# Gates of a hybrid encoder layer in three pieces, their tiles in the mixers' pool, and the decay rows stored through GpSimd's queue

## The chip, the cores and the metric

The kernel runs on one core of a Trainium2 chip. The metric is the device time of one execution in microseconds (us), the median of several. The engines are TensorE (PE, matmuls; PEld, its weight loads), VectorE (DVE), ScalarE (ACT), GpSimd (POOL) and SyncE (SP). Each engine works through its own instructions strictly in order; SP does nothing but issue DMA transfers, and GpSimd can issue them too.

## The reference

One layer of an encoder is computed for 1024 frames of a new stream (the prompt) and 32 frames of a running one (the sample), model width 1024, all in float32. What matters here is the input projection and what its gate columns feed:

```python
mod = jax.nn.silu(c) @ w_ada + b_ada                  # conditioning, 6 x 1024 columns
h = x * (1 + sc1) + sh1
mq, mk, mv, mo, mi, mf, fq, fk, fv, ff, gu, gv = split(h @ w_in)
li = mi + b_mlstm_i                                   # 4 heads
lf = log_sigmoid(mf + b_mlstm_f)                      # 4 heads
logf = log_sigmoid(ff + b_fox_f)                      # 8 heads, an output too
# forgetting attention (FoX), 8 heads of width 64
Ft = cumsum(logf, axis=1)
logits = q @ k.T * scale + Ft[query] - Ft[key]        # causal
hf = softmax(logits) @ v
# mLSTM, 4 heads, chunks of 64: running maxima m of b - b' + li, b = cumsum(lf)
w_intra = exp(dmat - m); w_inter = exp(m0 + b - m)
```

The mLSTM and the attention outputs join a gated MLP's, go through an output projection and a layer norm, then a SwiGLU feed-forward and another layer norm. Outputs besides the result are the attention's keys, values and log forgets, and the mLSTM's states C, n and m.

## The kernel before

Float32 products are made of two float32r parts: a weight tile `raw` (512 KB) is cast to `whi` on ACT (L105) and the rest `wlo` is formed on DVE (L106); each product then takes three matmuls (L117 to L119, and L282 to L284 with the operands' roles exchanged). Activations `h1h` and `h1l` are split likewise.

The program is written in one order, and a scheduler gives each engine its own, by when it expects an instruction's inputs and buffers to be there. First comes the conditioning (`ada`, L179: small matmuls, each unit with two loads of 512 KB into the two buffers `late`), the first projection, and two units of value columns (`tm_unit`) whose last 8 columns are the gate inputs, gathered in `G`. Then `gates()` runs, then a table `ORDER` names the rest of this stage: `q` is the projection of one attention head's queries and keys (`head_unit`, for heads 0 and 1 with further columns by `fm_unit`'s body), `f` is that head's attention on the first 512 rows, `k` the mLSTM's key projection, `v`, `o`, `a` further projections and conditioning units, `s` the mLSTM's states, `m` one mLSTM chunk. `f` and `m` have raised priority.

`gates()` does, in this order: a log-sigmoid on a tile of 128 partitions x 9 x 12 (DVE, a polynomial, with one ACT exp); four matmuls that make cumulative sums (L484 to L487); a matmul for the totals of earlier tiles (L497); the decay rows `fr`, 6 per head and tile, high and low parts and ones, stored to DRAM as `dfs` by two stores on SP; a running maximum in 7 steps (L512); a serial recurrence over 8 tiles (L525) between two tiny matmuls (L521 and L529); the columns `col` through four transposes (L547); and stores of `o_lf`, `dM`, `dd0` and the end states. Its tiles lie in a pool of their own, on the right of the memory, closed at its end. The pool `mx0`, of which the attention's and the mLSTM's tiles come, is opened after that.

A head's projection goes to one of three PSUM banks `g`. It is emptied by ACT and DVE into the tiles `qp`, `k1`, `k2`, `q2` (L399 to L404) and, for the output `o_kT`, through two small buffers `qkr` (L407; L368 and L424 use them too, and each waits until the store of an earlier user has landed). The tiles `q2` and `k2` get 4 rows each from `dfs` by loads on SP (`decay`). A score takes two matmuls: L768 needs the head's own tiles, L769 also the decay rows. L777 is the softmax's exp, L804 the transposes, L812 to L821 the products with the values.

Of the kernel before, what the change touches and what calls it, by code (L numbers as in the profile page):

```python
# [7 lines left out]
F32 = mybir.dt.float32  # L8
F32R = mybir.dt.float32r
AF = mybir.ActivationFunctionType  # L10
ALU = mybir.AluOpType
# [4 lines left out]
P = 128  # L16
# [4 lines left out]
NS = 32  # L21
# [14 lines left out]
T1 = (1, 1, 0, 2)  # L36
# [2 lines left out]
MLB = (1, 2, 3, 4, 5)  # L39
RESE = "pp"  # L40
TAFF = ("aaaaaaaa", "aaaaaaav")
ORDER = "q0 f0 q1 a f1 a q2 f2 k0 k1p s a q3 f3 a v q4 f4 a q5 f5 o a m0 q6 f6 a m1 q7 m2 f7 a m3"
ADAPOS = 4
GENG = (0, 1, 1, 0)
FP = (0, 0)
# [8 lines left out]
NEG = -1e30  # L54
# [11 lines left out]
def f(ap):  # L66
    return ap.bitcast(F32)


class Kernel:  # L70
# [10 lines left out]
    def t(self, pool, shape, dt=F32, tag=None, bufs=None):  # L81
        self.n += 1
        kw = {} if bufs is None else {"bufs": bufs}
        return pool.tile(shape, dt, tag=tag, name=f"{self.phase}_{tag}_{self.n}", **kw)
# [2 lines left out]
        self.lastload = self.nc.sync.dma_start(out, in_)  # L87
        return self.lastload

    def store(self, out, in_):  # L90
        self.nc.sync.dma_start(out, in_)


    def weights(self, src, nk, ncol, eng=None):
# [334 lines left out]
    def gates(self):  # L429
        self.phase = "gates"  # L430
        nc, d = self.nc, self.d
        ctx = ExitStack()
        gp = self.pool("gates", ctx=ctx, side="right")
        t = lambda shape, tag, dt=F32: self.t(gp, shape, dt, tag)
        R = 36
        ut = t([64, 64], "ut")
# [5 lines left out]
        ind, sel, back = t([R, 9], "ind"), t([R, 4], "sel"), t([4, R], "back")  # L442
# [10 lines left out]
        m0 = t([4, 9], "m0")  # L453
        nc.vector.memset(m0[:, 0:1], NEG)
        mm = t([4, 2, 9], "mm")
# [5 lines left out]
        a, e, s, s2, p = (t([P, 9, 12], f"g{i}") for i in range(5))  # L461
# [11 lines left out]
        ls = t([P, 9, 12], "ls")  # L473
# [3 lines left out]
        gi, gm, gn, gf = (t([P, 9, n], f"gw{i}") for i, n in enumerate((4, 4, 4, 8)))  # L477
# [11 lines left out]
        rf = t([72, P], "rf")  # L489
        nc.scalar.copy(rf, ps[:72, 256:384])  # L490
        nc.vector.tensor_copy(scan[0][:, 64:192], ps[:R, 0:128])
        rs = t([R, 4, P], "rs")
        nc.scalar.copy(rs[:, 0, :], ps[:R, 0:128])
        b = t([R, P], "gb")
# [3 lines left out]
        fc = t([64, 1], "fc")  # L498
        nc.vector.tensor_copy(fc, pc[:64, 0:1])
        ft = t([64, P], "ft")  # L500
# [3 lines left out]
        nc.vector.tensor_scalar(fr[:, 0:2, :], f(fr[:, 4:6, :]), -1.0, None, ALU.mult)  # L504
# [9 lines left out]
        E = t([R, 2], "E")  # L514
# [4 lines left out]
        EI = t([R, 2, 9], "EI")  # L519
        nc.vector.tensor_tensor(EI, E.unsqueeze(2).to_broadcast([R, 2, 9]), pair(ind), ALU.mult)  # L520
        nc.tensor.matmul(pc[:4, 32:50], sel, EI.rearrange("p a j -> p (a j)"), start=True, stop=True)  # L521
        ab = t([4, 2, 9], "ab")
        nc.vector.tensor_copy(ab, pc[:4, 32:50].rearrange("p (a j) -> p a j", a=2))
        for j in range(8):
            nc.vector.scalar_tensor_tensor(m0[:, j + 1:j + 2], ab[:, 0, j:j + 1], m0[:, j:j + 1], ab[:, 1, j:j + 1],  # L525
# [1 line left out]
        nc.vector.tensor_copy(mm[:, 0, 0:8], m0[:, 0:8])  # L527
        nc.vector.tensor_tensor(mm[:, 1, :], mm[:, 0, :], ab[:, 0, :], ALU.max)
        nc.tensor.matmul(pc[:R, 64:82], back, mm.rearrange("p a j -> p (a j)"), start=True, stop=True)  # L529
        mt, mc = t([R, 2, 9], "mt"), t([R, 2], "mc")  # L530
        nc.vector.tensor_tensor(mt, pc[:R, 64:82].rearrange("p (a j) -> p a j", a=2), pair(ind), ALU.mult)
        nc.vector.tensor_reduce(mc, mt, AX.X, ALU.add)
        M = t([R, P], "M")
# [4 lines left out]
        self.store(self.dM, M)  # L538
        self.store(d["o_m"], m0[:, 8:9])
        mes, d0 = t([4, 1], "mes"), t([4, 9], "d0")  # L540
        nc.vector.tensor_tensor(mes, mm[:, 1, 8:9], ab[:, 1, 8:9], ALU.add)
        self.store(d["o_ms"], mes)
        nc.vector.tensor_tensor(d0, mm[:, 0, :], mm[:, 1, :], ALU.subtract)
        self.store(self.dd0, d0)
# [757 lines left out]
    def run(self):  # L1302
        nc, tc, d = self.nc, self.tc, self.d
        dr = self.pool("dr", space=DRAM)
        t = lambda shape, tag: self.t(dr, shape, F32, tag)
# [60 lines left out]
        self.tm_unit(w1[0], 264, self.evac_v(0))  # L1366
        more(T1[1])
        self.tm_unit(w1[1], 264, self.evac_v(1))
        more(T1[2])
        self.gates()  # L1370
        more(T1[3])
        s2 = ExitStack()
        self.mx = self.pool("mx0", ctx=s2)
        self.foxbufs = (2, 2, 2, 2, 3)
        self.heads = {}

        def emit(x):
            eng = nc.gpsimd if x[-1] == "p" else nc.vector
            x = x.rstrip("p")
            i = int(x[1:] or 0)  # L1380
            if x[0] == "f":
                return self.fox(i, ((0, 1, 2, 3),))
            if x[0] == "m":
                return self.mlstm(i)
            if x[0] == "q":
                self.head_unit(i)
            elif x[0] == "k":
                self.fm_unit(w3[i], self.evac_mqk(2 + i, 0.125), eng=eng)
            elif x[0] == "s":
                self.mlstm_states()  # L1390
            elif x[0] == "a":
                more(1)
            else:
                self.tm_unit(w2["-vo".index(x)], 256, self.evac_raw((None, self.dmv, self.dmo)["-vo".index(x)]), eng=eng)
            return ()

        for x in ORDER.split():
            if x[0] in "fm" and HPA:
                with tc.high_priority(HPA):
                    weave(*[iter(emit(y)) for y in x.split("+")])  # L1400
            else:
                weave(*[iter(emit(y)) for y in x.split("+")])
# [119 lines left out]
        n = nj * 256  # L1522
        t = self.t(self.pz, [P, 4, n], F32R, "z0", 1)
        w = self.last_weights(((t[:, 0], t[:, 1]), (t[:, 2], t[:, 3])), (2, 3))
        act2 = dict(act)
        for half, (a, b) in enumerate(LN[1][::-1]):
# [6 lines left out]
            else:  # L1533
                h, l = (self.t(pb, [P, KT * 272], F32R, f"{x}{a}", 1) for x in ("ah", "al"))
# [111 lines left out]
```

## Time and profile before

| | |
|---|---|
| time, median of 3 runs (lowest, highest) | 1389.02 us (1388.13, 1390.63) |
| profiled execution: time, span | 1390.74 us, 1389.0 us |
| mean granted clock of TensorE | 0.988 |
| busy in the span: PE, DVE, ACT, POOL | 97%, 73%, 47%, 17% |
| where the stage stands in the span | first gate instruction on DVE (L459) at 108.66 us, projection of head 4 from 228.6 us on |

A row of the profile names line, engine, operation, output and input tiles without buffer numbers. "Granted clock" is the share of full speed that TensorE's throttle allowed. A busy PE sets the pace; idle time of another engine costs nothing unless PE waits for it.

### The profile page before, as it was taken

What the parts mean: (1) busy time and instruction counts of PE and PEld (TensorE: products, weight loads), DVE (VectorE), ACT (ScalarE), POOL (GpSimd) and SP (SyncE); (2) the same over time, 40 slices, a digit from 0 to 9 for tenths busy, and PEclk for the clock granted to TensorE, in tenths of its full rate; (3) what the DMA queues carried; (4) which work ended last, traced back from release to release, by engine and by line L of the source; (5) the groups of instructions that cost most, each with busy time, mean ns of one, the idle gap of its engine ahead of it and who ended that gap; (6) DMA issues with size and microseconds to landing.
All of it is one profiled execution on the core that took longest, in us unless ns stands there. A gap on an engine that the chain in (4) does not pass through costs nothing.

```text
span 1389.0 us, 25227 instructions
## 1 busy us (share of the span) xinstructions
PE 1341.3 (97%) x9432; PEld 1224.2 (88%) x9432; DVE 1013.7 (73%) x2144; ACT 653.7 (47%) x1274; POOL 236.2 (17%) x269
## 2 busy tenths in 40 slices
PE   7997999999999899999999999999999999999996
PEld 4896899988899778888887889899999999999996
DVE  5546643678779757777776766677998988888777
ACT  3313444553545544545544445345574554545355
POOL 1000100032156600000000000264610000000341
PEclk9999899999999999999999999999999999999998
DMA  9764664455765665444443442564597768463321
GB/s 360 252 225 122 187 186 129 128 170 157 224 202 159 171 199 182 125 131 137 135 134 86 107 127 80 187 171 133 160 239 188 214 165 212 139 175 112 102 91 65
DMA packets 123513, 224.65 MB, mean 162 GB/s; under 512 B 21260, under 2 KB 66232, under 8 KB 123392
## 3 DMA queue, kind: packets, MB, share of 16 engines
q1 hardware_dynamic: 118080, 212.95, 49.4%
q0 software_dynamic: 5168, 9.96, 4.6%
q8 instruction: 74, 1.21, 0.4%
q14 instruction: 47, 0.39, 0.1%
q10 hardware_dynamic: 144, 0.14, 0.0%
HBM read 191.21 MB, written 51.72 MB: 175 GB/s over the span
## 4 chain that ended last, share of the span: by engine, by line
PE 83%; DVE 7%; DMA 4%; ACT 2%; issue 2%; SPq 1%; POOL 1%; DVEq 0%; ACTq 0%; POOLq 0%
PE up_g L117 5%; PE up_g L118 5%; PE up_g L119 5%; PE dn_g L119 4%; PE dn_g L117 4%; PE dn_g L118 4%; PE sup_u L119 3%; PE sup_u L117 3%; PE sup_u L118 3%; PE tm_g L283 3%; PE tm_g L282 2%; PE tm_g L284 2%; PE wo_g L119 2%; PE wo_g L117 2%; PE wo_g L118 2%; PE fox_t L804 2%
## 5 line engine op out<-in xcount | busy, mean ns | idle before, releaser
L117 PE MATMUL up_g<-mlstm_ah,up_whi 128*128 128x512 f32 (+1 forms) x384 | 142.2, 371 | 5.1 <-ACT lna_tmp L1053 3.3
L118 PE MATMUL up_g<-mlstm_al,up_whi 128*128 128x512 f32 (+1 forms) x384 | 142.2, 370 | 0.4 <-DVE mlstm_al L1058 0.4
L119 PE MATMUL up_g<-mlstm_ah,up_wlo 128*128 128x512 f32 (+1 forms) x384 | 141.3, 368 | 0.0
L283 PE MATMUL tm_g<-tm_wlo,start_h1h 128*128 128x256 f32 (+1 forms) x384 | 109.4, 286 | 0.9 <-DVE tm_wlo L106 0.9
L282 PE MATMUL tm_g<-tm_whi,start_h1h 128*128 128x256 f32 (+1 forms) x384 | 109.1, 286 | 0.3 <-DVE tm_traw L352 0.2
L284 PE MATMUL tm_g<-tm_whi,start_h1l 128*128 128x256 f32 (+1 forms) x384 | 109.1, 285 | 0.0
L1177 ACT CAST sup_whi<-sup_raw 128x1024 fp32r<-128x1024 f32 x54 | 56.0, 1048 | 91.0 <-PE dn_u L118 47.6
L117 PEld LDWEIGHTS up_g<-mlstm_ah,up_whi 128*128 128x128 f32 x384 | 73.6, 192 | 17.5 <-ACT mlstm_ah L1057 3.5
L118 PEld LDWEIGHTS up_g<-mlstm_al,up_whi 128*128 128x128 f32 x384 | 73.7, 192 | 11.9 <-DVE mlstm_al L1058 1.1
L119 PEld LDWEIGHTS up_g<-mlstm_ah,up_wlo 128*128 128x128 f32 x384 | 73.8, 192 | 10.8
L777 ACT ACTIVATE fox_p<-fox_s,fox_fmx 128x384 f32<-128x384 f32 (+2 forms) x96 | 55.2, 579 | 57.2 <-DVE fox_fmx L775 43.6
L105 ACT CAST up_whi<-up_raw 128x1024 fp32r<-128x1024 f32 x50 | 52.4, 1048 | 61.6 <-PE dn_g L118 20.9
L1032 DVE SCALAR_TENSOR_TENSOR wo_z<-dn_g,start_mod,wo_z 128x512 f32<-128x512 f32 (+4 forms) x120 | 60.2, 519 | 22.5 <-PE dn_g L119 22.0
L1178 DVE TENSOR_TENSOR sup_wlo<-sup_raw,sup_whi 128x1024 fp32r<-128x1024 f32 x54 | 68.1, 1264 | 10.8 <-ACT sup_whi L1177 10.8
L106 DVE TENSOR_TENSOR up_wlo<-up_raw,up_whi 128x1024 fp32r<-128x1024 f32 x50 | 66.8, 1336 | 12.3 <-ACT up_whi L105 11.6
L283 PEld LDWEIGHTS tm_g<-tm_wlo,start_h1h 128*128 128x128 f32 x384 | 72.2, 188 | 2.6 <-issue 1.2
L282 PEld LDWEIGHTS tm_g<-tm_whi,start_h1h 128*128 128x128 f32 x384 | 72.1, 189 | 1.8 <-DVE tm_traw L352 0.7
L117 PE MATMUL dn_g<-up_acth,dn_whi 128*128 128x512 f32 (+2 forms) x200 | 73.5, 368 | 0.0
L118 PE MATMUL dn_g<-up_actl,dn_whi 128*128 128x512 f32 (+2 forms) x200 | 73.3, 368 | 0.0
L119 PE MATMUL dn_g<-up_acth,dn_wlo 128*128 128x512 f32 (+2 forms) x200 | 73.3, 366 | 0.0
L284 PEld LDWEIGHTS tm_g<-tm_whi,start_h1l 128*128 128x128 f32 x384 | 72.2, 188 | 0.5 <-issue 0.4
L105 ACT CAST dn_whi<-dn_raw 128x1024 fp32r<-128x1024 f32 (+1 forms) x44 | 42.7, 971 | 51.0 <-PE up_g L118 11.4
(641 smaller groups left out, 4605.5 us busy)
## 6 DMA issues: line engine op xcount, KB each, us to landing
up_raw<-w_gu SPq DMA_DIRECT2D x50, 512.0 KB
dn_raw<-w_dn SPq DMA_DIRECT2D x28, 512.0 KB
ada_late<-w_ada SPq DMA_DIRECT2D x24, 512.0 KB
wo_raw<-w_o SPq DMA_DIRECT2D x24, 512.0 KB
sup_raw<-w_gu SPq DMA_DIRECT2D x20, 512.0 KB
start_dp<-w_gu SPq DMA_DIRECT2D x19, 512.0 KB
start_dp<-w_gu POOLq DMA_DIRECT2D x19, 512.0 KB, 7.2
sup_raw<-start_dp SPq DMA_DIRECT2D x18, 512.0 KB
```

The lines of the kernel that those rows point to most:

```text
L105: nc.scalar.copy(hi[:, :w], raw[:, :w])
L106: (eng or nc.vector).tensor_tensor(lo[:, :w], raw[:, :w], f(hi[:, :w]), ALU.subtract)
L117: nc.tensor.matmul(ps, hi, xh(k), start=start and k == 0, stop=False)
L118: nc.tensor.matmul(ps, hi, xl(k), start=False, stop=False)
L119: nc.tensor.matmul(ps, lo, xh(k), start=False, stop=stop and k == n - 1)
L282: nc.tensor.matmul(ps[:, :ncol], xh, hi, start=k == 0, stop=False)
L283: nc.tensor.matmul(ps[:, :ncol], xh, lo, start=False, stop=False)
L284: nc.tensor.matmul(ps[:, :ncol], xl, hi, start=False, stop=k == 7)
L777: nc.scalar.activation(pr[:, lo:hi], banks[x][:, :hi - lo], AF.Exp, bias=mxs[:, 0:1], accum_out=sums[:, x:x + 1])
L1032: self.lastz = self.nc.vector.scalar_tensor_tensor(z[:, m, x:y], ps[:, x - a:y - a], g[i], z[:, m, x:y], ALU.mult, ALU.add)
L1177: nc.scalar.copy(h, x)
L1178: tt(l, x, f(h), ALU.subtract)
```

## The change

`gates()` becomes a generator in three parts. The first runs where `gates()` ran and ends with the decay rows; the second, the mLSTM's part, is named in `ORDER` as `g` behind head 0's attention; the third, with the stores of `o_lf`, `dM`, `dd0` and the end states, is a second `g` further back. The decay rows are two tiles now, queries and keys, stored by four DMAs on GpSimd's queue in place of two on SP's. The gates' tiles are taken from the mixers' pool `mx0`, under the names of mLSTM tiles (many small ones as slices of one tile `mo`), so that pool is opened before the gates.

```diff
-ORDER = "q0 f0 q1 a f1 a q2 f2 k0 k1p s a q3 f3 a v q4 f4 a q5 f5 o a m0 q6 f6 a m1 q7 m2 f7 a m3"
+ORDER = "q0 f0 g q1 a f1 a g q2 f2 k0 k1p s a q3 f3 a v q4 f4 a q5 f5 o a m0 q6 f6 a m1 q7 m2 f7 a m3"
...
-    def store(self, out, in_):
-        self.nc.sync.dma_start(out, in_)
+    def store(self, out, in_, eng=None):
+        (eng or self.nc.sync).dma_start(out, in_)
...
-        ctx = ExitStack()
-        gp = self.pool("gates", ctx=ctx, side="right")
-        t = lambda shape, tag, dt=F32: self.t(gp, shape, dt, tag)
+        t = lambda shape, tag, dt=F32, bufs=1: self.t(self.mx, shape, dt, tag, bufs)
+        few = t([64, 256], "mo")
...
-        scan = [t([R, 192], "scan0"), t([R, 192], "scan1")]
-        for x in scan:
-            nc.gpsimd.memset(x[:, 0:64], NEG)
-        fr = t([64, 6, P], "fr", F32R)
-        nc.gpsimd.memset(f(fr[:, 2:4, :]), 1.0)
+        scan = t([R, 2, 192], "mqb")
+        nc.gpsimd.memset(scan[:, :, 0:64], NEG)
+        scan = [scan[:, 0], scan[:, 1]]
+        fk = t([64, 4, P], "mqk", F32R)
+        nc.gpsimd.memset(f(fk[:, 2:4, :]), 1.0)
+        fq = t([64, 2, P], "mkw", F32R)
+        rows4 = t([72, 4, P], "mb")
+        rf, ft, b, M = rows4[:, 0], rows4[:64, 1], rows4[:R, 2], rows4[:R, 3]
...
-        x = t([P, 9, 16], "gx")
+        x = t([P, 9, 28], "mv1")
+        ls, x = x[:, :, 16:28], x[:, :, 0:16]
...
-        self.store(d["o_lf"].rearrange("(j p) h -> p j h", p=P), ls[:, 0:8, 4:12])
-        self.store(d["o_lfs"], ls[:NS, 8, 4:12])
...
-        nc.scalar.copy(fr[:, 4, :], ft)
-        nc.vector.tensor_tensor(fr[:, 5, :], ft, f(fr[:, 4, :]), ALU.subtract)
-        nc.vector.tensor_scalar(fr[:, 0:2, :], f(fr[:, 4:6, :]), -1.0, None, ALU.mult)
+        nc.scalar.copy(fq[:, 0, :], ft)
+        nc.vector.tensor_tensor(fq[:, 1, :], ft, f(fq[:, 0, :]), ALU.subtract)
+        nc.vector.tensor_scalar(fk[:, 0:2, :], f(fq), -1.0, None, ALU.mult)
         for r in (slice(0, 32), slice(32, 64)):
-            self.store(self.dfs[r], f(fr[r]))
+            self.store(self.dfs[r, 4:6], f(fq[r]), nc.gpsimd)
+            self.store(self.dfs[r, 0:4], f(fk[r]), nc.gpsimd)
         nc.vector.tensor_copy(self.sf[64:72, :], rf[64:72, 0:NS])
+        yield
+        self.phase = "gates"
+        pc = self.t(self.pt, [P, 512], F32, "t")
...
         nc.scalar.activation(self.col[:, :, 1:4, :], self.col[:, :, 1:4, :], AF.Exp)
-        ctx.close()
+        yield
+        self.store(d["o_lf"].rearrange("(j p) h -> p j h", p=P), ls[:, 0:8, 4:12])
+        self.store(d["o_lfs"], ls[:NS, 8, 4:12])
+        self.store(self.dM, M)
+        self.store(d["o_m"], m0[:, 8:9])
+        self.store(d["o_ms"], mes)
+        self.store(self.dd0, d0)
...
-        more(T1[2])
-        self.gates()
-        more(T1[3])
         s2 = ExitStack()
         self.mx = self.pool("mx0", ctx=s2)
+        more(T1[2])
+        gates = self.gates()
+        next(gates)
+        more(T1[3])
...
+            if x[0] == "g":
+                next(gates, None)
+                return ()
```

The lines of the changed program are up to 18 further down: L768, L769, L804 and L812 are L782, L783, L818 and L826 there, and the gates' L484, L497, L521, L529 and L547 are L496, L507, L534, L542 and L555.

On PE before, at the end of head 1's projection: `gates_t` are the gates' matmuls, `ada_t` two conditioning units, `fox_s` head 0's scores.

```order
L119 MATMUL fm_g_1711<-start_h1h_171,fox_wlo_1661 128x272
L521 MATMUL gates_t_1342<-gates_EI_1366,gates_sel_1280 4x18
L529 MATMUL gates_t_1342<-gates_mm_1293,gates_back_1281 36x18
L179 MATMUL ada_t_1407<-ada_late_1408,start_c_63_182 32x256 x4
L179 MATMUL ada_t_1407<-ada_late_1414,start_c_63_182 32x256 x4
L547 MATMUL gates_t_1399<-start_ident_121,gates_rs_1338 128x36 x3
L185 MATMUL ada_t_1407<-start_ident_121,ada_adas_1420 128x128 x2
L179 MATMUL ada_t_1429<-ada_late_1430,start_c_63_182 32x256 x4
L179 MATMUL ada_t_1429<-ada_late_1436,start_c_63_182 32x256 x4
L768 MATMUL fox_s_1579<-head_k_259_1460,head_qp_1462 128x128
L768 MATMUL fox_s_1590<-head_k_259_1460,head_qp_1462 128x256
L769 MATMUL fox_s_1579<-head_k_260_1461,head_q_262_1463 128x128
```

On PE now, around head 0's scores (`head_g_1642` is head 1's projection, `head_g_1894` head 2's; lines left out are more of the projections, the cumulative sums and the conditioning units):

```order
L119 MATMUL fm_g_1470<-start_h1h_171,ada_wlo_1386 128x272
L782 MATMUL fox_s_1508<-head_k_236_1389,head_qp_1391 128x128
L782 MATMUL fox_s_1519<-head_k_236_1389,head_qp_1391 128x256
L117 MATMUL head_g_1642<-start_h1h_169,gates_whi_1630 128x512
...
L179 MATMUL ada_t_1361<-ada_late_1368,start_c_63_182 32x256 x4
...
L119 MATMUL head_g_1894<-start_h1h_169,ada_wlo_1883 128x512
L783 MATMUL fox_s_1508<-head_k_237_1390,head_q_239_1392 128x128
L783 MATMUL fox_s_1519<-head_k_237_1390,head_q_239_1392 128x256
L117 MATMUL fm_g_2021<-start_h1h_169,fm_whi_2017 128x256
```

The scores' first matmuls stand ahead of head 1's projection, their second ones behind 96 projection matmuls of heads 1 and 2. The gates' matmuls L534, L542 and L555 stand some 100 to 190 rows behind L783.

On ACT before, from head 0's further columns (`fm_qkh_1532`) on: `head_g_1468` is head 0's bank, `gates_t` the gates'.

```order
L366 ACTIVATE fm_qkh_1532<-fm_g_1507,start_qsc_147 128x272
L105 CAST fm_whi_2041<-fm_raw_2039 128x1024
L366 ACTIVATE fm_qkh_1566<-fm_g_1541,start_qsc_147 128x272
L490 COPY gates_rf_1335<-gates_t_1330 72x128
L493 COPY gates_rs_1338<-gates_t_1330 36x128
L495 COPY gates_gb_1340<-gates_t_1330 36x128
L502 CAST gates_fr_1289<-gates_ft_1346 64x128
L182 COPY ada_adas_1420<-ada_t_1407 128x256
L399 ACTIVATE head_qp_1462<-head_g_1468 64x512
L399 ACTIVATE head_qp_1666<-head_g_1672 64x512
```

On ACT now, from the same place (`head_g_1397` is head 0's bank):

```order
L399 ACTIVATE head_qp_1391<-head_g_1397 64x512
L401 CAST head_k_236_1389<-head_g_1397 64x512
L366 ACTIVATE fm_qkh_1461<-fm_g_1436,start_qsc_147 128x272
L403 CAST head_k_236_1389<-head_g_1397 64x512
L404 ACTIVATE head_q_239_1392<-head_g_1397 64x512
L407 COPY head_qkr_1428<-head_g_1397 64x256
L407 COPY head_qkr_1431<-head_g_1397 64x256
L105 CAST fm_whi_2017<-fm_raw_2015 128x1024
L366 ACTIVATE fm_qkh_1495<-fm_g_1470,start_qsc_147 128x272
L501 COPY gates_mb_1287<-gates_t_1317 72x128
```

Head 0's bank is emptied ahead of the gates' copies instead of behind them and behind a conditioning unit.

On GpSimd now, around the stores of the decay rows (`mkw` and `mqk` are the tiles of the query and key rows):

```order
L368 TENSOR_TENSOR fm_qkr_1463<-fm_qkh_1461,fm_qkl_1462 128x272
L598 MEMSET mlstm_mv_586_3274 128x4
L368 TENSOR_TENSOR fm_qkr_1497<-fm_qkh_1495,fm_qkl_1496 128x272
L373 COPY start_qks_157<-fm_qkr_1497 128x32
L91 DMA start_dfs_64<-gates_mkw_1286 32x256 x2
L91 DMA start_dfs_64<-gates_mqk_1284 32x512 x2
L106 TENSOR_TENSOR fm_wlo_2136<-fm_raw_2133,fm_whi_2135 128x1024
```

And on SP now, where the loads of these rows stand (`head_q_239` and `head_k_237` are head 0's):

```order
L91 DMA start_dqh_57<-head_k_284_1634 64x512
L87 DMA ada_late_1362<-w_ada 128x1024
L87 DMA ada_late_1368<-w_ada 128x1024
L91 DMA start_dqh_57<-fm_qkh_1706 128x272
L91 DMA start_dql_58<-fm_qkl_1707 128x272
L87 DMA head_q_239_1392<-start_dfs_64 4x4x128
L87 DMA head_k_237_1390<-start_dfs_64 4x4x128
L87 DMA head_q_287_1637<-start_dfs_64 4x4x128
L87 DMA head_k_285_1635<-start_dfs_64 4x4x128
L91 DMA start_dql_58<-head_k_285_1635 64x512
L91 DMA start_dqh_57<-fm_qkh_1740 128x272
```

The stores stand on GpSimd behind the two adds for `o_kT` of head 0 and a memset. The loads stand on SP behind two conditioning loads and two stores of head 1, and five more stores of head 1 stand behind them, then the next conditioning and weight loads.

More of the change, by code (lines that the diff above doesn't have):

```diff
@@ L431, in gates, with small @@
         nc, d = self.nc, self.d
-        ctx = ExitStack()
-        gp = self.pool("gates", ctx=ctx, side="right")
-        t = lambda shape, tag, dt=F32: self.t(gp, shape, dt, tag)
+        t = lambda shape, tag, dt=F32, bufs=1: self.t(self.mx, shape, dt, tag, bufs)
+        few = t([64, 256], "mo")
+        at = [0]
+        def small(p, *dims):
+            n = 1
+            for x in dims:
+                n *= x
+            y = few[:p, at[0]:at[0] + n]
+            at[0] += n
+            return y.rearrange("p (a b) -> p a b", a=dims[0]) if len(dims) > 1 else y
         R = 36
-        ut = t([64, 64], "ut")
+        ut = small(64, 64)
         nc.gpsimd.memset(ut[:, 0:8], 0.0)
@@ L441, in gates @@
         rows = self.ident[:R, :R].rearrange("p (j h) -> p j h", h=4)
-        ind, sel, back = t([R, 9], "ind"), t([R, 4], "sel"), t([4, R], "back")
+        ind, sel, back = small(R, 9), small(R, 4), small(4, R)
         nc.vector.tensor_reduce(ind, rows, AX.X, ALU.add)
@@ L447, in gates @@
         pair = lambda x: x.unsqueeze(1).to_broadcast([R, 2, 9])
-        scan = [t([R, 192], "scan0"), t([R, 192], "scan1")]
-        for x in scan:
-            nc.gpsimd.memset(x[:, 0:64], NEG)
-        fr = t([64, 6, P], "fr", F32R)
-        nc.gpsimd.memset(f(fr[:, 2:4, :]), 1.0)
-        m0 = t([4, 9], "m0")
+        scan = t([R, 2, 192], "mqb")
[6 more added lines that the diff above has]
+        rf, ft, b, M = rows4[:, 0], rows4[:64, 1], rows4[:R, 2], rows4[:R, 3]
+        m0 = small(4, 9)
         nc.vector.memset(m0[:, 0:1], NEG)
-        mm = t([4, 2, 9], "mm")
+        mm = small(4, 2, 9)
         self.load(mm[:, 0, 8:9], d["state_m"])
-        x = t([P, 9, 16], "gx")
+        x = t([P, 9, 28], "mv1")
+        ls, x = x[:, :, 16:28], x[:, :, 0:16]
         nc.vector.tensor_tensor(x, self.G, self.rowp[:, 0:16].unsqueeze(1).to_broadcast([P, 9, 16]), ALU.add)
         z = x[:, :, 4:16]
-        a, e, s, s2, p = (t([P, 9, 12], f"g{i}") for i in range(5))
+        a, e, s, s2 = (y[:, i] for y in (t([P, 2, 9, 12], x) for x in ("mtot", "mhm")) for i in range(2))
+        p = t([P, 9, 12], "msq")
         nc.vector.scalar_tensor_tensor(a, z, -1.0, z, ALU.mult, ALU.min)
@@ L472, in gates @@
         nc.vector.tensor_scalar(a, z, 0.0, None, ALU.min)
-        ls = t([P, 9, 12], "ls")
         nc.vector.scalar_tensor_tensor(ls, p, -2.0, a, ALU.mult, ALU.add)
-        self.store(d["o_lf"].rearrange("(j p) h -> p j h", p=P), ls[:, 0:8, 4:12])
-        self.store(d["o_lfs"], ls[:NS, 8, 4:12])
-        gi, gm, gn, gf = (t([P, 9, n], f"gw{i}") for i, n in enumerate((4, 4, 4, 8)))
+        w = t([P, 180], "mixs", F32, 2)
+        gi, gm, gn, gf = (w[:, o:o + 9 * n].rearrange("p (j h) -> p j h", h=n)
+                          for o, n in ((0, 4), (36, 4), (72, 4), (108, 8)))
         nc.vector.tensor_copy(gf, ls[:, :, 4:12])
@@ L513, in gates @@
         A = scan[1][:, 64:]
-        E = t([R, 2], "E")
+        E = small(R, 2)
         nc.vector.tensor_copy(E[:, 0:1], A[:, P - 1:P])
@@ L518, in gates @@
         nc.vector.tensor_copy(E[32:, 1:2], b[32:, NS - 1:NS])
-        EI = t([R, 2, 9], "EI")
+        EI = small(R, 2, 9)
         nc.vector.tensor_tensor(EI, E.unsqueeze(2).to_broadcast([R, 2, 9]), pair(ind), ALU.mult)
         nc.tensor.matmul(pc[:4, 32:50], sel, EI.rearrange("p a j -> p (a j)"), start=True, stop=True)
-        ab = t([4, 2, 9], "ab")
+        ab = small(4, 2, 9)
         nc.vector.tensor_copy(ab, pc[:4, 32:50].rearrange("p (a j) -> p a j", a=2))
@@ L537, in gates @@
         nc.vector.tensor_scalar(rs[:, 3, :], rs[:, 0, :], mc[:, 1:2], None, ALU.subtract)
-        self.store(self.dM, M)
-        self.store(d["o_m"], m0[:, 8:9])
-        mes, d0 = t([4, 1], "mes"), t([4, 9], "d0")
+        mes, d0 = small(4, 1), small(4, 9)
         nc.vector.tensor_tensor(mes, mm[:, 1, 8:9], ab[:, 1, 8:9], ALU.add)
-        self.store(d["o_ms"], mes)
         nc.vector.tensor_tensor(d0, mm[:, 0, :], mm[:, 1, :], ALU.subtract)
-        self.store(self.dd0, d0)
         ps = self.t(self.pt, [P, 512], F32, "t")
```

10 lines of the change are left out of this document (3 added, 7 removed).

## Prediction

> **What bounds the kernel now.** I read the page's first two parts, then the stretches around the gate stage, then TensorE (PE) row by row, then the queues that feed it.
>
> ```profile
> PE 1341.3 (97%) x9432; PEld 1224.2 (88%) x9432; DVE 1013.7 (73%) x2144; ACT 653.7 (47%) x1274; POOL 236.2 (17%) x269
> 105.40:125.00 19.60, 19.60 (x116) 17.13 (x114) 13.26 (x42) 4.56 (x10) 0.00 (x0) 1.00 0.43 130
> 125.00:130.00 5.00, 2.90 (x21) 2.27 (x19) 2.87 (x15) 0.30 (x1) 0.00 (x0) 1.00 0.17 39
> 130.00:135.00 5.00, 2.25 (x23) 1.09 (x23) 4.13 (x18) 2.57 (x6) 0.64 (x2) 0.77 0.42 105
> 135.00:140.00 5.00, 1.31 (x12) 0.43 (x16) 1.47 (x3) 3.10 (x7) 0.00 (x0) 0.50 0.72 210
> 140.00:145.00 5.00, 5.00 (x27) 4.22 (x20) 2.93 (x9) 1.78 (x6) 1.71 (x3) 0.50 0.56 149
> 145.00:150.00 5.00, 5.00 (x28) 4.52 (x28) 2.66 (x8) 2.50 (x5) 1.45 (x2) 0.86 0.67 161
> 150.00:228.60 78.60, 77.41 (x608) 70.12 (x607) 37.50 (x94) 34.07 (x83) 2.73 (x3) 1.00 0.56 171
> 228.60:1389.00 1160.40, 1132.45 (x7872) 1045.32 (x7870) 894.14 (x1804) 574.35 (x1096) 223.09 (x232) 0.99 0.53 152
> ```
>
> The rows after the first are stretches: length, busy time of PE, PEld, DVE, ACT and POOL, the granted clock, the DMA share and GB/s. PE is busy 97% of the span, so PE's own time sets the end, except where it waits. From 125 to 140 us it is busy for 2.90, 2.25 and 1.31 of 5 us each: 8.54 us idle. In the same place the granted clock falls to 0.50 and is back at 1.00 only after 145 us. PE row by row, with the idle time before a row and its releaser in brackets:
>
> ```profile
> 105.45 0.40 PE L117 MATMUL head_g<-start_h1h,ada_whi 128*128 128x512 f32 x1
> 111.01 0.29 PE L117 MATMUL fm_g<-start_h1h,ada_whi 128*128 128x272 f32 x1
> 114.02 0.28 PE L117 MATMUL fm_g<-start_h1h,ada_whi 128*128 128x272 f32 x1
> 117.04 0.39 PE L117 MATMUL head_g<-start_h1h,fox_whi 128*128 128x512 f32 x1
> 127.69 0.20 PE L521 MATMUL gates_t<-gates_EI,gates_sel 36*4 36x18 f32 x2
> 130.36 0.24 PE L529 MATMUL gates_t<-gates_mm,gates_back 4*36 4x18 f32 x2 [2.47 <-DVE gates_mm L528]
> 130.86 1.07 PE L179 MATMUL ada_t<-ada_late,start_c 128*32 128x256 f32 x16 [0.26 <-DVE gates_mt L531]
> 135.86 1.08 PE L179 MATMUL ada_t<-ada_late,start_c 128*32 128x256 f32 x8 [2.99 <-DVE start_mod L197]
> 139.77 1.08 PE L179 MATMUL ada_t<-ada_late,start_c 128*32 128x256 f32 x8 [2.83 <-DMA ada_late<-w_ada]
> 141.80 0.43 PE L117 MATMUL fm_g<-start_h1h,fox_whi 128*128 128x272 f32 x1
> ```
>
> From 127.69 to 139.77 PE does the gates' little matmuls (L521, L529) and conditioning ones (L179), each behind a wait, and no projection. The first wait is for a serial recurrence on DVE; a third is for a load that SP could issue only after the L179 before it.
>
> ```profile
> 128.14 1.90 DVE L525 SCALAR_TENSOR_TENSOR gates_m<-gates_ab,gates_m 4x1 f32<-4x1 f32 x8
> 132.27 1.07 ACT L399 ACTIVATE head_qp<-head_g 64x512 fp32r<-64x512 f32 x2
> 127.14 0.78 SPq L91 DMA_DIRECT2D start_dfs<-gates_fr  x2
> 133.12 0.55 SPq L87 DMA_DIRECT2D ada_late<-w_ada  x1
> 133.72 0.32 SPq L87 DMA_DIRECT2D head_q<-start_dfs  x1
> ```
>
> ACT empties both heads' banks (L399) only at 132.27, though head 0's was full at 111; so PE has no third bank for more projections, and no scores either.
>
> **The change, part by part.** *The gap.* The 24 matmuls on 512 columns take 5.56 us (105.45 to 111.01), the 24 on 272 take 3.01 (111.01 to 114.02). In the new order ACT empties head 0 directly after its matmuls, and L521, L529 and L547 stand far back among the mLSTM projections and head 0's and 1's attention. The 8.54 us of idle time go. So does the half clock: busy time times the missing clock is 2.25 x 0.23 + 1.31 x 0.50 + 5.00 x 0.50 + 5.00 x 0.14 = 4.4 us. Gross: 12.9 us. No PE work of weight is added: the gates have the same matmuls in both orders.
>
> *What comes late next: the decay rows.* The first score matmul that needs them (L783 now, L769 before) stands after three more blocks of matmuls. PE ended head 1's first 48 projection matmuls at 127.69, gates' ones among them. Now add 0.4 for two score halves (half of their time at half clock), 3.01 for the last 24 on 272 columns, 5.56 for head 2's 24, two blocks of L179 at 1.07 and some 0.5 of transposes: PE comes to L783 at about 139.
>
> ```profile
> 126.69 0.28 DVE L504 TENSOR_SCALAR gates_fr<-gates_fr 64x256 fp32r<-64x256 f32 x1
> L1129 POOL DMA_DIRECT2D start_dp<-w_gu x19: 1026/1035/1522, 927.6 to 1228.2; - x19
> DMA to landing us min/median/max: 5.9/7.2/11.7
> 143.67 1.20 SPq L91 DMA_DIRECT2D o_kT<-fm_qkr  x2
> 145.70 0.37 ACT L407 COPY head_qkr<-head_g 64x256 f32<-64x256 f32 x1 [1.53 <-DMA o_kT<-fm_qkr]
> ```
>
> DVE had the rows ready at 126.97 (L504); now about 1.7 later, since the total's matmul stands 6 + 2 rows further back (1.2) and two scan steps stand between (0.5): the first pair at 128.2, the second at 128.7. GpSimd has issued DMAs only in L1129: 1.035 us each, so four are out at 132.3. Landing: a store of SP's took 2.0 (143.67 to 145.70, when ACT had its buffer back); GpSimd's took 5.9 to 11.7, but those move 512 KB from DRAM to DRAM, these 32 and 64 KB. I take 2.0, the row nearest in size: 134.3. SP loads the rows for head 0 then, another 2.0 and two issues of 0.3: 136.9. Two us are left, so this costs nothing; if that cover is gone, with 11.7 for the last, the rows are there at 146.6 and PE waits 7.6.
>
> [...] No run so far shows such a small store from GpSimd.
>
> Behind the waiting load on SP are stores of head 1, the next conditioning loads and weight loads, held from about 130 to 134.3; the nearest of them that PE needs is some 15 us off. Before GpSimd's stores stand two adds (L368) that wait for the landing of head 0's o_kT stores, issued at about 117; even with the 5.55 quoted below that is 122.5, some 4 us early. Between them stands a memset of an mLSTM tile (L598) that waits until the store of o_lf has read the gates' tile there; that store too is issued at about 117, and has 11 us for its landing, which no row shows.
>
> *The conditioning load.* The second L179 block needs loads that SP issues after the first has run, at about 129. The row of 133.12 landed at 139.77, 6.65 later; with that PE, there at about 134 and 136.4, waits up to 1.7. Below it is nothing. I take 0.5.
>
> *The buffers of keys.* Head 2's and the mLSTM's outputs leave through two small buffers (qkr), each given back when its store has landed:
>
> ```profile
> 165.40 0.39 PE L117 MATMUL fm_g<-start_h1h,fm_whi 128*128 128x272 f32 x1 [1.13 <-ACT head_qkr L407]
> 166.76 5.55 DMA o_kT<-head_qkr
> 172.39 0.32 ACT fm_qkr L424
> 156.37 2.23 DMA mlstm_mb<-start_dM
> ```
>
> PE waited 1.13 for that now, and ACT 5.55 once for one landing, with PE covered. With PE 12 us ahead, and its clock full, the cover is thinner: 1.1 to 5.5; I take 3.0. *The last part's wait*: an early piece of mLSTM on DVE reads dM broadcast, behind a store and a load (2.23 for the load now); DVE stands for up to 3 us, with PE some 1.5 short of it; 0 to 1.5, I take 0.5.
>
> *Gate tiles in the mixers' pool*: the first mLSTM block takes these tiles over from the gates' last stores, and only its early piece on DVE, priced above, is near: nothing more. *Stores last*: the two log-forget outputs and three others are off the path.
>
> Sum: 12.9 gross; waits 0.5 + 0 + 3.0 + 0.5 = 4.0, in place of the 1.19 idle that 150 to 228.6 has now (78.60 - 77.41): 12.9 - 2.8 = 10.1 us. After 228.6, where head 4's projection begins, PE's instructions stand in the same order in both, and PE is 97.6% busy there with DMA at 0.53, so the lead is kept. The profiled execution took 1390.74 (span 1389.0), 1.7 over the median; the gain is taken off the median: 1389.0 - 10.1 = **1378.9 us**.
>
> **The rivals.** *The buffers set the pace.* If o_kT landings of 5.55 us come at each turn, PE waits 5.5 around the mLSTM projections, and the clock falls again. For: the row of 166.76. Against: other landings took 2. Price of the clock: a mean of 0.86 over 145 to 150 puts its return at 146.4, so from 139.77 PE worked 6.6 us without a pause at half: 3.3 lost. Gain 12.9 + 1.2 - 5.5 - 3.3 - 1.0 = 4.3: 1384.7. Chance 0.18. [...]
>
> *GpSimd's stores come too late* (slower). It decides from the point where PE waits at L783 so long that, with 3.3 for the clock, the net 10.1 is gone: 6.8 us, rows at 145.8. With 1.522 for each issue (134.3) and 11.7 for the last landing, the stores are down at 146.0, the rows at 148.6: 9.6 + 3.3 against 10.1, slower by 2.8: 1391.8. For: the only DMAs of GpSimd's in the trace are that slow. Against: they are 8 to 16 times as large. Chance 0.11.
>
> *No difference*: the decay loads come 6 to 7 us late by the same path and eat the lead, or a later stage gives it back: 1389. Against the latter, DMA at 0.53. Chance 0.07. The forecast has 0.64.
>
> **How the numbers follow.** The forecast's own range goes from waits of 1.1 in all (gain 13.0: 1376.0) to 1.7 + 5.5 + 1.5 = 8.7 (gain 5.4: 1383.6). The range reaches to the first rival: 1375.5 to 1385.5, leaving out the last two (0.18). About 0.2%, 2.8 us, is what a measurement of this kernel can tell from no change. Faster: 0.64 + 0.18 = 0.82; same 0.07; slower 0.11.
>
> **What would show it.** Right: PE without idle time over 1 us from 117 to 139, granted clock 1.00 through 150, head 4's projection starting near 218 instead of 228.6. Wrong: a wait at L783 for the loads from dfs (late stores), a second fall of the clock, or ACT's L424 waiting 5 us for o_kT with PE behind it. The prediction fails as a whole if head 4 starts early and the end does not move.

## The result, and the profile after

The changed kernel took 1379.13 us (median of 5; 1377.83 to 1383.65) against 1389.02 beside it: a ratio of 0.9936, 95% interval 0.9919 to 0.9952. It is faster by 9.9 us; the forecast was 1378.9, with a range of 1375.5 to 1385.5.

The stage is best measured from the start of head 0's projection to the start of head 4's, since each execution reaches head 0 at another time (104.3 to 106.5) and the profiled execution after is the slowest of its five (1383.65 us). The window before, and then the one after; the columns are length, PE, PEld, DVE, ACT, POOL, the granted clock, DMA share and GB/s:

```profile
105.45:228.57 123.12, 113.38 (x824) 99.70 (x823) 64.82 (x185) 48.80 (x116) 6.54 (x9) 0.94 0.53 157
```

```profile
104.62:217.29 112.67, 111.16 (x825) 97.14 (x823) 60.01 (x185) 48.97 (x116) 10.48 (x13) 1.00 0.55 169
```

The stage is 10.45 us shorter (123.12 to 112.67). PE's idle time in it (length less busy) went from 9.74 to 1.51, its busy time from 113.38 to 111.16, and the mean clock from 0.94 to 1.00. In slices, after:

```profile
125.00:130.00 5.00, 5.00 (x47) 4.11 (x47) 2.46 (x12) 1.47 (x4) 2.20 (x4) 1.00 0.53 111
130.00:135.00 5.00, 5.00 (x32) 3.55 (x30) 1.90 (x6) 2.59 (x4) 2.39 (x1) 1.00 0.60 223
135.00:140.00 5.00, 5.00 (x36) 4.04 (x36) 1.63 (x5) 2.96 (x9) 1.87 (x3) 1.00 0.62 150
140.00:145.00 5.00, 5.00 (x42) 4.92 (x41) 4.20 (x16) 1.84 (x6) 0.72 (x1) 1.00 0.67 224
145.00:150.00 5.00, 4.42 (x32) 3.69 (x32) 4.41 (x14) 4.28 (x12) 0.00 (x0) 1.00 0.75 270
150.00:217.30 67.30, 66.37 (x526) 58.91 (x525) 31.22 (x96) 27.37 (x67) 0.60 (x1) 1.00 0.53 165
```

Where PE was busy for 2.90, 2.25 and 1.31 of 5 us it is now busy for all 5, and the clock stays at 1.00. ACT empties the banks of heads 0 and 1 as soon as each is full:

```profile
110.38 0.59 ACT L399 ACTIVATE head_qp<-head_g 64x512 fp32r<-64x512 f32 x1 [1.62 <-PE head_g L119]
123.38 0.59 ACT L399 ACTIVATE head_qp<-head_g 64x512 fp32r<-64x512 f32 x1 [0.33 <-PE head_g L119]
```

They stood at 132.27 before, both together. Three of PE's rows: head 0's first scores with decay rows, a wait in head 0's transposes, and head 4's projection (before at 228.57):

```profile
138.11 0.39 PE L783 MATMUL fox_s<-head_k,head_q 68*128 68x128 f32 x2
147.15 0.33 PE L818 MATMUL fox_t<-start_ident,fox_p 128*128 128x128 f32 x1 [0.55 <-DVE fox_p L799]
217.29 0.40 PE L117 MATMUL head_g<-start_h1h,tm_whi 128*128 128x512 f32 x1
```

L783 runs without a wait. The longest wait of PE in the stage, from the list of waits, is a new one:

```profile
PE ada_t L185 <- ACT ada_adas L182: 0.9, 1, 0.9
```

The queues of GpSimd and SP carry the decay rows, and the list of DMA issues from 126 to 130 us gives (last column) the median time from issue to landing:

```profile
127.10 1.23 POOL L91 DMA_DIRECT2D start_dfs<-gates_mkw  x2 [6.59 <-DVE gates_mo L530]
128.31 0.99 POOL L91 DMA_DIRECT2D start_dfs<-gates_mqk  x2
...
133.38 0.28 SPq L87 DMA_DIRECT2D head_q<-start_dfs  x1
133.71 0.29 SPq L87 DMA_DIRECT2D head_k<-start_dfs  x1
```

```profile
start_dfs<-gates_mqk POOLq DMA_DIRECT2D x2, 64.0 KB, 5.0
start_dfs<-gates_mkw POOLq DMA_DIRECT2D x2, 32.0 KB, 5.6
```

The last store went out at 128.80 and was down at 133.77. SP issued head 0's loads at 133.38 and 133.71, when its own two stores had landed.

### The profile page after: what moved, and what is told of

Its sections match the earlier page's. It is cut to its first block, busy times and chain, and to the rows that moved or that the text cites. A ratio compares the mean times of both kernels' runs of the same rounds, so it can differ in the third digit from the quotient of the medians.

```text
span 1381.0 us, 25237 instructions
## 1 busy us (share of the span) xinstructions
PE 1340.4 (97%) x9432; PEld 1222.8 (89%) x9432; DVE 1008.3 (73%) x2144; ACT 653.7 (47%) x1274; POOL 242.6 (18%) x272
## 4 chain that ended last, share of the span: by engine, by line
PE 84%; DVE 8%; DMA 3%; ACT 2%; issue 1%; POOL 0%; SPq 0%; DVEq 0%; ACTq 0%; POOLq 0%
PE up_g L117 5%; PE up_g L118 5%; PE up_g L119 5%; PE dn_g L119 4%; PE dn_g L117 4%; PE dn_g L118 4%; PE sup_u L119 3%; PE sup_u L117 3%; PE sup_u L118 3%; PE tm_g L283 2%; PE tm_g L282 2%; PE tm_g L284 2%; PE wo_g L119 2%; PE wo_g L117 2%; PE wo_g L118 2%; PE fox_t L818 2%
## 5 line engine op out<-in xcount | busy, mean ns | idle before, releaser
L283 PE MATMUL tm_g<-tm_wlo,start_h1h 128*128 128x256 f32 (+1 forms) x384 | 109.5, 286 | 0.9 <-DVE tm_wlo L106 0.9
L106 DVE TENSOR_TENSOR up_wlo<-up_raw,up_whi 128x1024 fp32r<-128x1024 f32 x50 | 66.6, 1333 | 9.6 <-ACT up_whi L105 8.9
```

The source lines that it names most:

```text
L106: (eng or nc.vector).tensor_tensor(lo[:, :w], raw[:, :w], f(hi[:, :w]), ALU.subtract)
L283: nc.tensor.matmul(ps[:, :ncol], xh, lo, start=False, stop=False)
```

## The experiments

Each kernel below was run beside the kernel before, and its ratio has a 95% interval. The stage is the same stretch of the program in each, from head 0's projection to head 4's; where no other view is named, a row that begins with two times is that stage.

**The changed kernel again** (no edit).

> The changed kernel once more, for a second profiled execution and as the measure for the three beside it. In the first execution its lead over before, matmul by matmul, was 11.9 us at 149, 11.3 at 280 and 8.0 at the end; the 3.3 went between 290 and 473 us at places where PE waits in both kernels (L620, L117 of fm_g, L179 of ada_g), half of it as half clock. Theory (the position of the clock's falls changes from execution to execution, the waits do not): the same waits, but other falls, a lead at the end anywhere from 8 to 11.5 us, median 1377 to 1381. Rival (the later loss belongs to the changed program): the lead falls by 3 us again, at the same places.

Measured: 1377.64 us, ratio 0.9930 (0.9914 to 0.9945). Its stage, and what follows head 4's start, and then what follows it in the first execution after and in the one before:

```profile
104.31:216.82 112.51, 111.18 (x825) 97.15 (x823) 59.91 (x185) 49.17 (x116) 10.48 (x13) 1.00 0.56 169
216.82:1362.82 1146.00, 1130.88 (x7872) 1044.26 (x7870) 885.56 (x1783) 568.71 (x1087) 222.85 (x232) 1.00 0.52 153
```

```profile
217.29:1369.44 1152.15, 1134.31 (x7872) 1046.67 (x7870) 886.24 (x1783) 569.11 (x1087) 221.82 (x232) 0.99 0.53 152
```

```profile
228.57:1377.52 1148.95, 1132.47 (x7872) 1045.35 (x7870) 885.82 (x1783) 569.23 (x1087) 223.09 (x232) 0.99 0.53 152
```

The stage took 112.51, as in the first execution (112.67). Behind head 4 the same program took 1146.00 here and 1152.15 there, with the kernel before at 1148.95 between them. So the 3.3 us that the first profile lost after 290 is no property of the program: 3.43 of the 6.15 between its two executions are busy time (17.1 us at half clock there, 10.2 here), 2.72 are waits. The theory holds, and its range was too narrow: matmul by matmul, the lead at the end was 14.7 us here, 8.1 there (1.1 and 0.8 of it stand at head 0 already). The stage is the measure that the rest goes by.

**The decay rows through SP again.**

```diff
-            self.store(self.dfs[r, 4:6], f(fq[r]), nc.gpsimd)
-            self.store(self.dfs[r, 0:4], f(fk[r]), nc.gpsimd)
+            self.store(self.dfs[r, 4:6], f(fq[r]))
+            self.store(self.dfs[r, 0:4], f(fk[r]))
```

> The decay rows' four stores go back to SP's queue; all else as changed. Theory of the prediction (the queue is worth nothing, since the rows have about 2 us in hand at L783): within 1 us of the changed kernel, 1378 to 1380, no wait at L783, and stores that land in some 2 to 3 us. Rival (SP's stores, waiting for DVE at about 127, hold back the conditioning load issued behind them, and PE waits for it): L179 waits 2 to 4 us, 1381 to 1384.

Measured: 1378.47 us, ratio 0.9932 (0.9919 to 0.9946).

```profile
106.01:217.83 111.82, 111.32 (x824) 97.28 (x823) 60.61 (x185) 49.27 (x116) 7.44 (x9) 1.00 0.57 170
```

The stage is 0.69 to 0.85 shorter than with GpSimd's queue, with no wait at L783 nor at L179. GpSimd's queue brings nothing here.

**The pool alone.** The gates run in one piece where they did before, and the stores go through SP; only the tiles stay in the mixers' pool.

```diff
-ORDER = "q0 f0 g q1 a f1 a g q2 ...
+ORDER = "q0 f0 q1 a f1 a q2 ...
...
-        next(gates)
+        for _ in gates:
+            pass
```

> As the one before, and the stores on SP's queue too: of the change only the move of the tiles to the mixers' pool is left. Theory A (the pool alone): 1378 to 1382, the gap gone. Theory B (the split): 1385 to 1389, waits at L534 and L542. If the queue matters only with the undivided gates, this one is slower than the one with GpSimd's stores by the wait at L783, 1 to 4 us.

Measured: 1378.55 us, ratio 0.9930 (0.9916 to 0.9943).

```profile
106.04:218.69 112.65, 111.27 (x825) 97.57 (x823) 62.35 (x185) 49.08 (x116) 8.00 (x9) 1.00 0.55 169
```

The stage is 112.65 us long, within 0.14 of the whole change's in two executions. Theory A holds in the time: of the three parts of the change the move of the tiles is enough for all of the gain. Its reason, that the heads' tiles lay on the gates' memory, is the subject of the next kernel. PE's order shows the projection of head 2 ahead of L542 even with the gates in one piece, and ACT empties head 0 at 111.80. The third part, the last stores named further back, changes nothing at all: with the second `g` put directly behind the first, every engine's instructions stand in the same order, so that kernel was not run.

**The same, and two heads made to share memory with the gates.**

```diff
-        rows4 = t([72, 4, P], "mb")
+        rows4 = t([72, 4, P], "qp", F32, 2)
...
-        rs = t([R, 4, P], "mw")
+        rs = t([R, 4, P], "qp", F32, 2)
```

> The kernel with the pool's move alone (gates in one piece, stores on SP), with one thing more: the gates' two late-living tiles (rows4 and rs) take the two buffers named qp that heads 0 and 1 need for their queries. All gate tiles still lie in the mixers' pool; only these two heads must wait for the gates again. Theory (the gap comes from memory that the heads' evacuations share with the gates, not from the gates' place in the program): the gap is back, 8 us idle between 125 and 140, the granted clock at 0.5 there, L399 of both heads at about 132, 1386 to 1389. Rival (another property of the pool's move, such as the order of pools or the freed right side, made the gain): as with the pool's move alone, 1377 to 1380.

Measured: 1384.88 us, ratio 0.9980 (0.9966 to 0.9994). The stage, ACT's row for the two heads, and PE's longest waits:

```profile
106.16:224.53 118.37, 111.76 (x825) 99.21 (x823) 62.91 (x185) 48.50 (x116) 6.70 (x9) 0.96 0.52 158
```

```profile
133.08 1.07 ACT L399 ACTIVATE head_qp<-head_g 64x512 fp32r<-64x512 f32 x2 [0.39 <-DMA start_dM<-gates_qp]
```

```profile
PE ada_t L179 <- DMA ada_late<-w_ada: 3.5, 2, 2.9
PE gates_t L542 <- DVE gates_mo L541: 2.3, 1, 2.3
```

PE's instructions of this stage stand nearly in the order of the kernel before again, the clock is at half from 133.2 to 143.4, and ACT empties both heads at 133.08, named by the profile as behind the store of dM, which reads the gates' tile in that buffer. So memory that the gates still hold is enough to make a gap. Of the 10.5 us it brings back 5.7 (118.37 against 112.65); why not all was not tried. The median is 1.1 us below what was expected.

The kernel before made its gap in another way. In its trace L399 names no wait; it follows the row ahead of it on ACT at once:

```profile
132.00 0.37 ACT L182 COPY ada_adas<-ada_t 128x256 f32<-128x256 f32 x1 [5.66 <-PE ada_t L179]
```

By the addresses that the built program gives its tiles, those of heads 0 and 1 lay at bytes 79776 to 100256 of a partition and the gates' at 124096 to 137956: they shared none. Only the pool as a whole, `mx0` at 79776 to 137536, reached into the gates' part. When these heads' tiles get a pool of their own at the same addresses, opened in the same place, and the gates stay as they were, the scheduler's order has head 0's L399 ahead of the gates' copies (a program that was built and not run). So in the kernel before it was the order of ACT that put L399 late. It points to a scheduler that held back these tiles because another part of their pool lay on the gates' memory; what that program would take in time is not shown.

**Gates in one piece, stores through GpSimd** (the edit of the pool alone, with `nc.gpsimd` kept).

> The gates are emitted in one piece where they were before, with their tiles in the mixers' pool and the stores on GpSimd's queue. The order of PE's instructions then has the projection of head 2 ahead of L542 and L783 even so. Theory A (the pool alone removes the gap: head 0's and 1's banks can be emptied at once because their tiles no longer lie on the gates' memory): no idle over 1 us on PE from 117 to 139, clock 1.00, head 4's projection within 2 us of the changed kernel's 217.3, 1378 to 1382. Theory B, as the prediction put it (naming the mLSTM's part behind head 0 is what clears the gap): waits at L534, L542 or L555 of 2 to 3 us each come back, the clock falls, 1385 to 1389.

Measured: 1385.54 us, ratio 0.9984 (0.9974 to 0.9994). The stage, and PE's one long wait:

```profile
104.65:224.21 119.56, 115.96 (x824) 99.20 (x823) 63.71 (x185) 49.05 (x116) 10.19 (x13) 0.97 0.52 159
```

```profile
150.99 0.60 PE L179 MATMUL ada_t<-ada_late,start_c 128*32 128x256 f32 x1 [2.71 <-DVE start_mod L197]
```

Theory A, which expected 1378 to 1382, missed: the old gap is gone, with no wait over 1 us before 148, but a new one costs most of the gain. Theory B has the time and names the wrong wait, since nothing stops at L534, L542 or L555. Of the 6.9 us that the stage is longer than with stores on SP (119.56 against 112.65), 2.2 are idle and 4.7 are busy time, 2.3 of these for half clock from 148.71 to 155.54. With stores on GpSimd the scheduler's order is another one: the second conditioning unit stands closer to the first, and PE waits 2.71 there. So GpSimd's queue is not free in itself: with undivided gates it costs 7 us of the median, and naming the mLSTM's part behind head 0 gives these back.

**The same, and L581 held back on ACT.** In the kernel above ACT waits at L581 for a load, with L399 and L182 behind it:

```profile
146.27 0.22 ACT L581 ACTIVATE fm_d0c<-fm_d0c 128x18 f32<-128x18 f32 x1 [5.57 <-DMA fm_d0c<-start_dd]
```

```diff
-        nc.scalar.activation(self.d0c, self.d0c, AF.Exp)
+        z = self.t(self.cst, [P, 1], F32, "z")
+        nc.vector.tensor_scalar(z, f(self.lastk[:, 0:1]), 0.0, None, ALU.mult)
+        nc.scalar.activation(self.d0c, self.d0c, AF.Exp, bias=z)
```

`lastk` is the tile `k1` of head 2.

> The kernel with gates in one piece and stores on GpSimd's queue, which took 1385.5, and in it the exp of d0c (L581 on ACT) made to depend on head 2's keys, so that ACT runs it behind head 2's evacuation (L399, L401) instead of before it; PE's order is unchanged. Theory (ACT waits 5.57 us at L581 for the load of dd0 while L399 and L182 stand behind it; the conditioning chain L182, L185, L197 comes late, and PE waits 2.7 at L179 and then works at half clock): ACT has no wait over 3 us at this place, PE none over 1.5 between 145 and 151, 1378 to 1381. Rival (PE waits for the late conditioning load itself, issued at 145.6 on SP): the wait at L179 stays, 1383 to 1386.

Measured: 1381.91 us, ratio 0.9959 (0.9944 to 0.9975). The stage, PE's wait, and SP's two loads of the unit:

```profile
105.90:225.09 119.19, 115.64 (x825) 99.31 (x824) 64.00 (x186) 49.21 (x116) 10.00 (x13) 0.97 0.53 160
```

```profile
151.70 0.61 PE L179 MATMUL ada_t<-ada_late,start_c 128*32 128x256 f32 x1 [3.55 <-DMA ada_late<-w_ada]
```

```profile
145.31 0.38 SPq L87 DMA_DIRECT2D ada_late<-w_ada  x1
146.25 0.38 SPq L87 DMA_DIRECT2D ada_late<-w_ada  x1
```

The theory fell for the stage: ACT runs L399 (L400 in this kernel) at 145.17 now and waits for no load there, yet PE waits even longer, and for the conditioning load by name. SP issued the unit's first half at 145.31, and PE went on 6.39 later. Without the edit SP issued it at 144.67 and PE went on at 150.99, 6.32 later. There the last part of that load landed at 150.86, and L197, which the row names, ended at 150.87:

```profile
150.72 0.15 DVE L197 TENSOR_SCALAR start_mod<-start_mod 128x4 f32<-128x4 f32 x1
```

So there load and chain held PE equally long, and with the chain early the load still does. The stage is as long as without the edit (119.19 and 119.56). The median is 3.6 us lower all the same, and behind head 4 this execution was the shortest of all (1143.5); whether L581 has a share in that stays open.

**GpSimd's stores held back.** Eight, four and six adds on GpSimd ahead of the stores:

```diff
+        for i in range(8):
+            nc.gpsimd.tensor_tensor(fk[:, 2:4, :], f(fq), f(fk[:, 2:4, :]) , ALU.add)
+        nc.gpsimd.memset(f(fk[:, 2:4, :]), 1.0)
```

> The changed kernel with GpSimd held up ahead of its stores of the key rows by eight adds on 64 x 256 elements, which change nothing in what is stored: the rows reach DRAM some 4 to 6 us later, so 2 to 4 us after the point where L783 stood at 138.1. The scheduler knows of the adds and puts L783 25 matmuls (some 3.5 us) further back. Theory (only PE's wait counts, and there is other work to put first): within 1.5 us of the changed kernel, 1377 to 1380.5, wait at the score matmul below 1.5. Rival of the prediction (rows that come late cost a wait and the clock): a wait of 2 to 6 us there, the clock at 0.5 behind it, 1382 to 1388.

Measured: 1388.08 us, ratio 0.9998 (0.9985 to 1.0011). The stage, the two stores of key rows, and PE's wait at the score matmul (L786 here):

```profile
106.14:226.55 120.41, 114.00 (x824) 100.19 (x823) 62.21 (x185) 49.07 (x116) 15.71 (x22) 0.97 0.52 158
```

```profile
139.89 1.01 POOL L91 DMA_DIRECT2D start_dfs<-gates_mqk  x2 [0.30 <-POOL gates_mqk L516]
```

```profile
146.39 0.30 PE L786 MATMUL fox_s<-head_k,head_q 68*128 68x128 f32 x1 [3.52 <-DMA head_k<-start_dfs]
```

The edit held the rows back more than meant: a weight split (L106) came between the adds, and the key rows were down at 144.36, 10.6 us later than in the changed kernel. PE waited 3.52 for them although the scheduler had put L786 26 matmuls further back, and the whole gain is gone from the median (the stage is still 2.7 shorter than before). The rival's mechanism is real.

> As with eight adds ahead of GpSimd's key-row stores, but four. With eight, the key rows were stored at 139.89, had landed at 144.36, the load issued at 144.54 was there at 146.39, and PE, which came to the score matmul at 142.87, waited 3.5. Four adds fewer take 3.14 from that: rows there at about 143.2. PE's order is the same as with eight. Theory (it decides at the point where the rows are there when PE comes): a wait of 0 to 0.5 us, no fall of the clock between 140 and 165, 1377 to 1380.5. Rival (any delay of the rows is passed on, since what follows on SP and ACT is late too): 1381 to 1385.

Measured: 1385.11 us, ratio 0.9976 (0.9964 to 0.9987).

```profile
106.47:224.29 117.82, 113.67 (x824) 98.85 (x823) 61.60 (x185) 49.17 (x116) 12.72 (x18) 0.99 0.54 162
```

```profile
144.23 0.46 PE L786 MATMUL fox_s<-head_k,head_q 68*128 68x128 f32 x2 [1.03 <-DMA head_k<-start_dfs]
151.41 0.39 PE L785 MATMUL fox_s<-head_k,head_qp 128*128 128x256 f32 x1 [1.28 <-ACT fox_p L794]
```

> As before, with six adds: rows there at about 144.8, a wait of 1.5 to 2 us at the score matmul. [...] Rival (the price jumps to that of eight adds, some 9 us, once PE waits at all): 1385 to 1388.

Measured: 1386.41 us, ratio 0.9987 (0.9972 to 1.0002).

```profile
104.59:225.79 121.20, 115.72 (x824) 101.06 (x823) 61.62 (x185) 49.21 (x116) 14.22 (x20) 0.96 0.52 157
```

```profile
144.15 0.47 PE L786 MATMUL fox_s<-head_k,head_q 68*128 68x128 f32 x2 [2.83 <-DMA head_k<-start_dfs]
```

With four adds the wait is 1.03, and the stage is already 5.2 us longer than after (117.82). The theory expected no loss there, and the rival is right: what follows is late too, PE waits for ACT's exp between two heads (1.28), and the clock falls for one stretch of 3.40. With six the wait is 2.83 and the stage 121.20: again the rival, a jump to the price of eight adds. Most of the loss is there with the first microsecond of waiting. That the later place of the scores on PE has a share in it, beside the wait, is argued, not shown.

## Why the prediction was right

*The gap.* Its 8.54 us of idle went entirely, as said, and head 4 began at 217.29 against "near 218". The working named the order of ACT and the far place of L521, L529 and L547 for it; the runs show what is behind that order. The prediction priced the move of the tiles as one that costs "nothing more" and gave it no share in the gain. It is the whole gain: the time came out right with the part of the change that makes it left unnamed.

*Half clock.* The term of 4.4 us was too large: PE's busy time in the stage fell by 2.2. The half clock itself cost 3.9 before (half of the 7.84 us for which PE was busy from 132.72 to 146.38); but the same 822 matmuls, at full clock throughout, take 111.2 to 111.3 in the three kernels without the gap, and with that loss taken off 109.5 before and 108.4 in the kernel with shared memory (111.76 less 3.4). So the mixed order has 1.7 to 2.9 us more busy time. What makes it is not shown.

*New waits.* 4.0 was too much as well: idle time in the stage after is 1.51. The buffers of keys, priced at 3.0, made PE wait for nothing here (1.4 in the kernel with the pool alone, inside the range of 1.1 to 5.5). The conditioning load cost 0 instead of 0.5, and dM 0 instead of 0.5: DVE waited 4.7 for it at L615, and PE did not. L185 behind ACT (0.9) was not foreseen. Idle fell by 8.2 where 5.7 were forecast, busy time by 2.2 where 4.4 were: the sum, 10.45 against 10.1, is right partly because two mis-sized terms cancel.

*GpSimd's stores.* Costing nothing was right, with about 2 us in hand: in the kernel with eight adds a load issued at 144.54 let PE go at 146.39, 1.85 later, so after the change the rows were there at an estimated 135.6 (133.77 and 1.85), 2.5 before L783. But the terms were off: the stores took 0.50 to 0.69 to issue, not 1.035, and 5.0 to 5.9 to land, not 2.0. The last was down at 133.77 against 134.3, and the four landed 0.2 to 0.4 apart. With the gates in one piece the same stores on GpSimd's queue took 2.0 and 2.5, near the 2.0 that was taken, in the list from 126 to 130 us:

```profile
start_dfs<-gates_mqk POOLq DMA_DIRECT2D x2, 64.0 KB, 2.0
start_dfs<-gates_mkw POOLq DMA_DIRECT2D x2, 32.0 KB, 2.5
```

SP issued no load of 512 KB from 124 to 131 us there; after the change it had issued two at 126.75. Whether these two made the stores slower is not shown.

*After 228.6.* The lead is kept in the median (9.9 in both comparisons), and moves by several us from one execution to the next (8.1 and 14.7 at the end of the two profiled ones).

*The rivals.* The buffers did not set the pace. GpSimd's stores were in time by 2.5 us; when they are 10.6 late, no gain is left (1388.1 with rows at 146.4; the rival had 1391.8 for rows at 148.6). The lead did not get lost later. The price of the clock in the first rival, 3.3 by the row, lies among the 1.5 to 3.9 that single falls cost, below.

## What to carry to other kernels

When an engine empties a buffer long after it was filled and waits for nothing in the trace, ask which pool the destination comes from and on whose memory any part of that pool lies: a pool opened over a closed one ordered work here that had neither data nor bytes in common. Of a change in several parts, run each part alone before a gain is put down to the one with the best story; here the tiles' move alone, a much smaller edit, is as good as the whole, and one of the other parts did harm without its companion. Slack is no price: rows so late that PE waited 1.0 us for them, with the order that the scheduler then chose, cost the stage 5.

## What was not expected of the hardware

The clock falls and returns in steps of one length. Slices of 1 us at the fall and the return, before, and in the kernel with eight adds:

```profile
132.00:133.00 1.00, 0.87 (x5) 0.44 (x5) 0.47 (x3) 1.00 (x3) 0.00 (x0) 0.86 0.33 47
146.00:147.00 1.00, 1.00 (x8) 1.00 (x7) 0.00 (x0) 0.44 (x2) 0.00 (x0) 0.81 0.76 264
```

```profile
146.00:147.00 1.00, 0.61 (x4) 0.64 (x5) 0.28 (x2) 0.00 (x0) 0.00 (x0) 0.87 0.05 16
150.00:151.00 1.00, 1.00 (x10) 1.00 (x9) 0.00 (x0) 0.00 (x0) 0.61 (x2) 0.92 0.31 78
```

A slice's mean of 0.86 puts the fall at 132.72, and 0.81 the return at 146.38: 13.66 us. The other two give 146.74 and 150.16: 3.42. In all eleven profiles, the 34 stretches at half clock between 100 and 560 us last 3.40 to 3.42 or two, three or four times that. Within one execution the falls also stand a whole number of such steps apart: before, those at 132.72, 375.06, 470.64 and 511.60 are 71, 28 and 12 steps from one to the next. What makes the clock fall is not shown. In the step ahead of 31 of these falls PE was busy for 3 to 62%, and in that ahead of the other three for all of it. From 105 us to the fall at 132.72 PE's longest wait was 2.47 us. The busy share alone does not decide either. Two steps ahead of the fall before:

```profile
125.90:129.31 3.41, 2.00 (x15) 1.68 (x15) 1.87 (x9) 0.30 (x1) 0.00 (x0) 1.00 0.25 58
129.31:132.72 3.41, 2.09 (x23) 1.09 (x23) 2.69 (x15) 0.72 (x2) 0.64 (x2) 1.00 0.03 5
```

The clock stayed up after the first, with PE busy for 59%, and fell after the second, with 61%; in another place it stayed up after 45% (L581 held back, from 470.61). In these 34 stretches it returned only after steps of 86% or more, and twice not: after 94% (before, from 139.55) and 88% (four adds, from 467.68). So one fall cost from 1.5 us of work (the changed kernel again, at 363.35) to 3.9 (before), by how many steps it lasted and how full they were. The two executions of the changed kernel lost 8.1 and 4.4 us to half clock after 100 us (10.0 before). Why one program's falls differ between its executions is not shown.
